# Hybrid attention/HGRN2 layer: per-head weight blocks for queries and keys, and attention taken one block at a time with the scores two blocks ahead

## The chip, the core and the metric

The kernel runs on one core of one Trainium2 chip. The metric is the device time of one execution in microseconds (us). The kernel before was run three times: 1170.23, 1170.86 and 1172.86 us, a median of 1170.86 us.

## What is computed

One layer on 1024 tokens of width 1024, in float32. Only the first half of it matters here:

```python
u = rms_norm(x, norm1_g)
aq, ak, av, hq, hf, hi, hg = split(u @ w_in)     # each 1024 x 512
attn = dilated_attention(aq, ak, av)             # 8 heads of 64
rec  = hgrn2_mixer(hq, hf, hi)                   # 4 recurrent heads of 128
h = x + concat(norm(attn), norm(rec) * silu(hg)) @ w_out
out = rms_norm(h + conv_glu(rms_norm(h)))
```

The attention has three causal windows merged by their softmax denominators: the last 128 keys, every fourth of the last 512, every sixteenth of the last 2048. For a block of 128 queries that is one softmax over up to 256 near keys (the block and the one before) and the far keys of the query's own residue modulo 4 (32 per earlier block), with a mask that carries the logarithm of how often a key is counted.

## The kernel before, in words

Every large product is made of three float32r matmuls: weights and activations are split into a high part (a cast on ScalarE, L87) and a low part (a subtraction on VectorE, L89), and high*high, high*low and low*high are added in PSUM (L492 to L494). The weights come through a ring (class `Ring`): a raw tile is loaded by a DMA on SyncE's queue, split, and used up by one step of 12 matmuls; five steps are kept ahead. Two 128-row blocks of `w_qk` together with two halves of the tokens are multiplied in seven steps instead of eight (Strassen-Winograd form): `PairMix` makes the weight sums on VectorE, `pair_block` (L511) runs the seven steps through two PSUM banks with the tag "mm" and adds their results into four tiles from `mtile` (tag "m", four buffers).

Only TensorE's order is written out by hand (`manual_schedule`); the other engines' orders are chosen by a scheduler when the program is built. TensorE is interleaved like this. `qk_block(0)` runs first. The other three pairs of heads, and the first HGRN2 projections (`early`, L784), are generators in `fill`; each `fill.run(us)` emits about so many us of their matmuls between pieces of the attention. For each pair of heads p (four of them) and each block b of 128 queries (eight):

- `scores(p, b)` (L690): 16 or 32 small matmuls into two PSUM banks S (one per head), then for each head the row minimum of mask minus scores with its write to P (VectorE, L715), the exponential with its sum (ScalarE, L717), the reciprocal (VectorE, L718) and the division (GpSimd, L719). P has two buffers per head.
- `turn(p, b)` (L724): transposes of P on TensorE into banks Tn and Tf of the tag "t" (L734, L742), copied out by ScalarE (pl, L735) and VectorE (far_t and tri, L745 and L748).
- `values(p, hf)` (L750), once per four blocks: the products with v into a bank O.

Blocks go in twos: scores of two blocks, values if four are complete, some fill, turn, fill, turn, fill. PSUM has eight banks: two each of "o", "t", "s" and "mm". Even blocks put their scores into "s" and "s", odd ones into "t" and "o". After the last block `fill.run()` empties what is left.

Queries and keys are laid out by `evac` (L632): each finished tile of a qk block holds one head, 64 rows of queries over 64 rows of keys. VectorE scales it by the norm of its tokens (L636), then ScalarE copies its two halves into the tiles qp and kp (L638), reordered so that within a block of 128 tokens those of one residue modulo 4 lie together. Four tiles per pair make 32 such copies in all.

`restore` (L776) reloads a quarter of x into four `mtile`s and rebuilds the operand T4, which the second half of `early` needs.

The functions around the change, with the line numbers of the profile:

Of the kernel before, what the change touches and what calls it, by code (L numbers as in the profile page):

```python
# [10 lines left out]
F32 = mybir.dt.float32  # L11
# [6 lines left out]
P = 128  # L18
SEQ = 1024
DM = 1024  # L20
NCT = DM // P
H2 = 512
NH = 8
# [4 lines left out]
KS = 4  # L28
# [111 lines left out]
class PairMix:  # L140


    def __init__(self, nc, a, b):
        self.nc, self.a, self.b, self.g0, self.g1 = nc, a, b, None, None

    def load(self, ring):
        self.g0, self.v0, self.v1 = ring.raw(self.a[:, 0:H2]), ring.raw(self.b[:, 0:H2]), ring.raw(self.b[:, H2:])

    def a11(self, ring):
        self.load(ring)  # L150
# [8 lines left out]
        return self.s  # L159

    def a12(self, ring):
        self.g1 = ring.raw(self.a[:, H2:])
        return self.g1

    def s3(self, ring):
# [81 lines left out]
def hybrid_kernel(ctx: ExitStack, tc: tile.TileContext, xT, w_qk, w_tok, w_hg, w_out, w_up,  # L247
                  w_down, vecs, amask, hmask, out):
    nc = tc.nc
    PE, DVE, ACT, POOL = nc.tensor, nc.vector, nc.scalar, nc.gpsimd  # L250
# [29 lines left out]
    halves = [slice(0, H2), slice(H2, SEQ)]  # L280
# [47 lines left out]
    def part(f, i):  # L328
        return w_up[f, :, H2 * i : H2 * (i + 1)]

    for f in range(NFF):
        if f < 2:
            plan += [((x, f), part(f, i)) for x, i in (("a11", 0), ("a12", 3), ("a21", 1), ("a22", 2))]
        else:
            m = Mix(nc, w_up[f])
# [3 lines left out]
    ring = Ring(nc, ringp, plan)  # L339
# [37 lines left out]
    R1 = ua.tile([P, SEQ], F32, name="R1")  # L377
# [10 lines left out]
    def bank(tag, name):  # L388
        return ps1.tile([P, H2], F32, tag=tag, name=name, bufs=2)
# [4 lines left out]
    at = at_cm.__enter__()  # L394
# [6 lines left out]
    ring.aside = {("a12", 1): None}  # L401

    def mtile(name):
        return at.tile([P, H2], F32, tag="m", name=name, bufs=4)

    def otile1(name):
        return at.tile([P, H2], F32, tag="ot", name=name, bufs=1)
# [6 lines left out]
    xp = xp_cm.__enter__()  # L414
# [8 lines left out]

    pin = tc.keep_in_program_order
    xt = {(hf, c): xs[hf][c // 2][:, (c % 2) * H2 : (c % 2 + 1) * H2] for hf in range(2) for c in range(KS)}
    xt |= {(0, KS + c): mtile(f"x21_{c}") for c in range(KS)}
    xt |= {(1, KS + c): xp.tile([P, H2], F32, name=f"x22_{c}") for c in range(KS)}
    OPS1 = ("B11", "B21", "T4", "B22")

# [136 lines left out]
    fill = Fill()  # L566
# [48 lines left out]
    for t in TURN:  # L615
        x = vtile(f"it{t}")
# [6 lines left out]
    qk = {}  # L623

    def by_residue(ap):
        return ap.rearrange("p (b l r) -> p b r l", l=32, r=4)

    def in_order(ap):
        return ap.rearrange("p (b r l) -> p b r l", l=32, r=4)

    def qk_evac(p):
        def evac(m, hf, src):  # L632
            if p not in qk:
                qk[p] = [at.tile([P, SEQ], F32, tag=x, name=f"{x}{p}", bufs=2) for x in ("qp", "kp")]
            t, r0 = halves[hf], 64 * m
            DVE.tensor_mul(src, src, R1[:, t])  # L636
            for dst, y in zip(qk[p], (slice(0, 64), slice(64, 128))):
                ACT.copy(in_order(dst[r0 : r0 + 64, t]), by_residue(src[y]))  # L638
        return evac

    def qk_block(p):
# [2 lines left out]
    FAR, NEAR = 192, 256  # L644
# [11 lines left out]
    ab = ab_cm.__enter__()  # L656
# [2 lines left out]
    tri = ab.tile([P, 2, 2, P], F32, name="tri")  # L659
    if True:  # L660
        nat = far_t.rearrange("p e b q -> p (e b q)")
        sel = ab.tile([P, FAR + NEAR], F32, tag="P0", name="sel", bufs=2)
        scratch = drv.tile([P, FAR + NEAR], F32, name="scratch")
        nat1 = ab.tile([P, FAR + NEAR], F32, tag="P1", name="nat1", bufs=2)
        nc.scalar.dma_start(nat1[:, 0:NEAR], amask[:, SEQ - NEAR :])
        nc.scalar.dma_start(nat[0:32, 0:768], amask[0:P:4, 0:768])
        POOL.tensor_scalar(in_order(sel[:, FAR:]), by_residue(nat1[:, 0:NEAR]), DH ** 0.5, 0.0, op0=ALU.mult, op1=ALU.add)
# [12 lines left out]
        def load_values(p, kb):  # L680
            near_v[p, kb] = ab.tile([P, 4, P], F32, tag="near", name=f"near{p}_{kb}", bufs=2)
            far_v[p, kb] = ab.tile([P, 4, P], F32, tag="far", name=f"far{p}_{kb}", bufs=2)
            src = vd[H2 * kb : H2 * (kb + 1), P * p : P * (p + 1)]
            for r in range(4):
                nc.sync.dma_start(near_v[p, kb][32 * r : 32 * r + 32], src.rearrange("(b l r) e -> r l b e", b=4, r=4)[r])
            nc.sync.dma_start(far_v[p, kb], src.rearrange("(p r) e -> p r e", r=4))
# [3 lines left out]
        def scores(p, b):  # L690

            qp, kp = qk[p]
            far = 32 * max(b - 1, 0)
            near = P if b == 0 else 2 * P
            k0 = (b + 1) * P - near
            n = far + near
            S = [bank(("to" if b % 2 else "ss")[e], f"S{p}_{b}_{e}") for e in range(2)]
            rows = [slice(64 * e, 64 * e + 64) for e in range(2)]
            k4 = kp.rearrange("p (b r l) -> p r b l", r=4, l=32)
            for part in range(2 if far else 1):  # L700
                for r in range(4):
                    o = slice(32 * r, 32 * r + 32)
                    for e in range(2):
                        q = qp[rows[e], b * P + 32 * r : b * P + 32 * r + 32]
                        if part == 0:
                            PE.matmul(S[e][o, far:n], q, kp[rows[e], k0 : k0 + near], start=True, stop=True)
                        else:
                            PE.matmul(S[e][o, 0:far].rearrange("p (b l) -> p b l", l=32), q,  # L708
                                      k4[rows[e], r, 0 : b - 1], start=True, stop=True)
            m = mask[:, FAR - far :] if b else mask[:, FAR + P :]  # L710
            Ps = probs[p, b] = []
            for e in range(2):
                Pt = ab.tile([P, FAR + NEAR], F32, tag=f"P{e}", name=f"P{p}_{b}_{e}", bufs=2)
                st = at.tile([P, 16], F32, tag="st", name=f"st{p}_{b}_{e}", bufs=8)
                DVE.tensor_tensor_reduce(Pt[:, :n], S[e][:, :n], m, -(DH ** -0.5), BIG * 3,  # L715
                                         op0=ALU.add, op1=ALU.min, accum_out=st[:, 0:1])
                ACT.activation(Pt[:, :n], Pt[:, :n], AF.Exp, bias=st[:, 0:1], scale=-1.0, accum_out=st[:, 2:3])  # L717
                DVE.reciprocal(st[:, 3:4], st[:, 2:3])  # L718
                POOL.tensor_scalar(Pt[:, :n], Pt[:, :n], st[:, 3:4], 1.0, op0=ALU.mult, op1=ALU.mult)  # L719
                Ps.append(Pt)  # L720
# [72 lines left out]
                if hf == 0:  # L793
                    restore()

        scores(0, 0)
        scores(0, 1)
        fill.add(early())
        us = 18.6
        ends = []  # L800
        for p in range(NH // 2):
            for j in range(4):
                if p or j:
                    for b in range(2):
                        scores(p, 2 * j + b)
                    while ends:
                        values(*ends.pop())
                if j == 0:
                    for kb in range(2):
                        load_values(p, kb)  # L810
                turns = [lambda b=b: turn(p, 2 * j + b) for b in range(2)] + [lambda: None]
                for n, f in zip(((3, 1, 1), (3, 2, 1), (2, 2, 1), (4, 3, 1))[j], turns):
                    fill.run(us / 24 * n)
                    f()
                if p == 3 and j == 3:
                    fill.run()
                if j % 2:
                    ends.append((p, j // 2))
        values(*ends.pop())
    ab_cm.__exit__(None, None, None)  # L820
    at_cm.__exit__(None, None, None)
# [2 lines left out]
    with pool("hg", "right") as hg:  # L824
# [95 lines left out]
        for hf in range(2):  # L920
            for kind, h in HG[0]:
                x = tile_of(kind, h, hf)
# [418 lines left out]
    with pool("ps2", "left", space=PSUM) as ps2:  # L1341
# [162 lines left out]
        for x, y in STAGES:  # L1504
# [27 lines left out]
            for d in range(KS):  # L1532
                src = ps[d]
# [89 lines left out]
```

## Time and profile before

| what | value |
| --- | --- |
| the profiled execution's own time | 1171.42 us |
| its span, first to last instruction | 1169.3 us |
| median of the three runs | 1170.86 us |
| TensorE matmuls, busy | 1145.6 us (98%) |
| weight loads, busy | 941.8 us (81%) |
| VectorE, busy | 923.7 us (79%) |
| ScalarE, busy | 604.3 us (52%) |
| GpSimd, busy | 87.5 us (7%) |
| chain that ended last | TensorE 86%, VectorE 7%, ScalarE 5% |
| the 32 copies of L638, busy | 17.8 + 18.1 us (in 95 to 282 us) |

A matmul of 512 columns is booked as busy for 0.39 us, but in a full stream the next one starts 0.23 us later; busy times of TensorE therefore overlap, and an idle time in the record begins only when the last booked time is over. The attention is the stretch from about 117 us (end of the first qk block) to 282.5 us (the end of the last values). In an idle entry such as `10.3 <-POOL P L719 5.1` the first number is the idle time ahead of a group of instructions, and what follows is the instruction whose end let it go on. DMA issues stand under SPq and ACTq, the queues of the engines that issue them.

### The profile page before, as it was taken

What the parts mean: (1) busy time and instruction counts of PE and PEld (TensorE: products, weight loads), DVE (VectorE), ACT (ScalarE), POOL (GpSimd) and SP (SyncE); (2) the same over time, 40 slices, a digit from 0 to 9 for tenths busy, and PEclk for the clock granted to TensorE, in tenths of its full rate; (3) what the DMA queues carried; (4) which work ended last, traced back from release to release, by engine and by line L of the source; (5) the groups of instructions that cost most, each with busy time, mean ns of one, the idle gap of its engine ahead of it and who ended that gap; (6) DMA issues with size and microseconds to landing.
All of it is one profiled execution on the core that took longest, in us unless ns stands there. A gap on an engine that the chain in (4) does not pass through costs nothing.

```text
span 1169.3 us, 17983 instructions
## 1 busy us (share of the span) xinstructions
PE 1145.6 (98%) x6472; PEld 941.8 (81%) x6472; DVE 923.7 (79%) x1728; ACT 604.3 (52%) x1149; POOL 87.5 (7%) x111
## 2 busy tenths in 40 slices
PE   9999899999999999999999999999999999999996
PEld 7887677778888888888788888888888888888886
DVE  7776667645876786759989998899888879857987
ACT  6545677654976665546434343434343344444553
POOL 5210122221000001120000000000000000000000
PEclk9999999999999999999999999999999999999998
DMA  6225121424212243340123333223322277435532
GB/s 245 87 67 165 38 92 47 129 81 147 91 55 64 72 155 124 110 135 27 55 89 101 117 127 108 81 100 117 117 90 83 97 255 250 135 99 162 168 106 88
DMA packets 84617, 130.90 MB, mean 112 GB/s; under 512 B 8432, under 2 KB 27664, under 8 KB 84528
## 3 DMA queue, kind: packets, MB, share of 16 engines
q1 hardware_dynamic: 70240, 105.08, 28.4%
q10 hardware_dynamic: 14288, 24.67, 5.6%
q8 instruction: 51, 0.84, 0.3%
q14 instruction: 38, 0.31, 0.1%
HBM read 98.63 MB, written 31.09 MB: 111 GB/s over the span
## 4 chain that ended last, share of the span: by engine, by line
PE 86%; DVE 7%; ACT 5%; issue 1%; DMA 1%; POOL 0%; ACTq 0%; SPq 0%; DVEq 0%; POOLq 0%
PE p L1224 10%; PE p L1223 10%; PE p L1222 10%; PE ds L1521 3%; PE ds L1523 3%; PE ds L1522 3%; PE po L492 3%; PE po L493 2%; PE po L494 2%; PE da L1521 2%; PE da L1523 2%; PE da L1522 2%; PE phq L492 1%; PE phg L492 1%; PE v L494 1%; PE phq L494 1%
## 5 line engine op out<-in xcount | busy, mean ns | idle before, releaser
L87 ACT CAST whi<-raww 128x512 fp32r<-128x512 f32 x246 | 150.5, 617 | 208.7 <-PE p L1223 69.0
L89 DVE TENSOR_TENSOR wlo<-raww,whi 128x512 fp32r<-128x512 f32 x247 | 173.1, 702 | 47.0 <-ACT whi L87 43.5
L87 ACT CAST whi<-r 128x512 fp32r<-128x512 f32 x70 | 43.6, 622 | 81.3 <-PE ds L1522 49.0
L89 DVE TENSOR_TENSOR wlo<-r,whi 128x512 fp32r<-128x512 f32 x70 | 48.0, 687 | 18.5 <-ACT whi L87 18.4
L1223 PE MATMUL p<-b1l,whi 128*128 128x512 f32 x160 | 62.3, 389 | 0.0
L1521 PE MATMUL ds<-fhi,whi 128*128 128x512 f32 x160 | 62.3, 389 | 0.0
L1522 PE MATMUL ds<-flo,whi 128*128 128x512 f32 x160 | 62.3, 389 | 0.0
L1224 PE MATMUL p<-b1h,wlo 128*128 128x512 f32 x160 | 62.3, 389 | 0.0
L1523 PE MATMUL ds<-fhi,wlo 128*128 128x512 f32 x160 | 62.3, 389 | 0.0
L1222 PE MATMUL p<-b1h,whi 128*128 128x512 f32 x160 | 62.3, 389 | 0.0
L89 DVE TENSOR_TENSOR flo<-rawf,fhi 128x512 fp32r<-128x512 f32 x70 | 48.0, 686 | 4.0 <-ACT fhi L87 3.9
L87 ACT CAST fhi<-rawf 128x512 fp32r<-128x512 f32 x70 | 43.1, 616 | 14.5 <-DMA rawf<-spT 5.8
L1495 POOL TENSOR_TENSOR facc<-facc,sqf 128x256 f32<-128x256 f32 x2 | 1.5, 739 | 637.3 <-ACT sqf L1494 637.3
L1251 ACT ACTIVATE cv<-cv 128x512 f32<-128x512 f32 x44 | 27.8, 632 | 40.6 <-DVE cv L1244 40.5
L1244 DVE SCALAR_TENSOR_TENSOR cv<-g,vec,cv 128x511 f32<-128x511 f32 (+2 forms) x92 | 44.7, 492 | 4.5 <-ACT cv L1241 4.2
L719 POOL TENSOR_SCALAR P<-P,st 128x128 f32<-128x128 f32 (+7 forms) x64 | 37.7, 591 | 132.8 <-DVE st L718 123.2
L1521 PE MATMUL da<-fhi,whi 128*128 128x512 f32 x120 | 46.7, 389 | 0.0
L1522 PE MATMUL da<-flo,whi 128*128 128x512 f32 x120 | 46.7, 389 | 0.0
L1523 PE MATMUL da<-fhi,wlo 128*128 128x512 f32 x120 | 46.7, 389 | 0.0
L717 ACT ACTIVATE P<-P,st 128x128 f32<-128x128 f32 (+7 forms) x64 | 35.7, 558 | 19.2 <-DVE st L715 19.0
L715 DVE CUSTOM_DVE_ANT_0 P<-S,mask 128x128 f32<-128x128 f32 (+7 forms) x64 | 30.0, 489 | 6.5 <-PE S L708 5.9
L1222 PEld LDWEIGHTS p<-b1h,whi 128*128 128x128 f32 x160 | 30.0, 188 | 6.3
(608 smaller groups left out, 3445.0 us busy)
## 6 DMA issues: line engine op xcount, KB each, us to landing
raww<-in_w_up_dram SPq DMA_DIRECT2D x88, 256.0 KB, 2.9
rawf<-spT SPq DMA_DIRECT2D x40, 256.0 KB, 2.7
r<-in_w_down_dram SPq DMA_DIRECT2D x40, 256.0 KB, 3.2
raww<-in_w_out_dram SPq DMA_DIRECT2D x32, 256.0 KB, 2.7
spB<-a ACTq DMA_DIRECT2D x30, 256.0 KB, 2.2
spT<-t ACTq DMA_DIRECT2D x30, 256.0 KB, 2.0
rawf<-spB SPq DMA_DIRECT2D x30, 256.0 KB, 2.7
raww<-in_w_hg_dram SPq DMA_DIRECT2D x24, 256.0 KB, 2.6
```

The lines of the kernel that those rows point to most:

```text
L87: self.pin(self.high(hi[:, :w], raw))
L89: self.pin(low.tensor_sub(lo[:, :w], raw, f32(hi[:, :w])))
L492: PE.matmul(ps, a[0], b[0], start=start, stop=False)
L494: PE.matmul(ps, a[1], b[0], start=False, stop=stop)
L719: POOL.tensor_scalar(Pt[:, :n], Pt[:, :n], st[:, 3:4], 1.0, op0=ALU.mult, op1=ALU.mult)
L1222: PE.matmul(ps, hi[:, s], bhi, start=(start and n == 0), stop=False)
L1223: PE.matmul(ps, hi[:, s], blo, start=False, stop=False)
L1224: PE.matmul(ps, lo[:, s], bhi, start=False, stop=(stop and n == len(rhs) - 1))
L1244: DVE.scalar_tensor_tensor(dst, x, col(V_CW + j * NFF + f), dst, op0=ALU.mult, op1=ALU.add)
L1521: PE.matmul(ps[d], hi[:, s], ahi, start=(k == 0), stop=False)
L1522: PE.matmul(ps[d], hi[:, s], alo, start=False, stop=False)
L1523: PE.matmul(ps[d], lo[:, s], ahi, start=False, stop=(k == NPAIR - 1))
```

## The change

It has two parts. In the first, each raw tile of `w_qk` is put together from two blocks, 64 columns of each (`PairMix.part`): its four 128-column groups hold one half of block a beside the same half of block b, so that a finished tile holds the queries of both heads of a pair, or the keys of both. Every tile is loaded by two DMAs in pieces of 256 bytes where it was one DMA with 2 KB per partition. `evac` then is one VectorE multiplication that reads in order and writes qp or kp in the reordered layout; the ScalarE copies go.

In the second, the attention goes block by block. The scores of blocks 0 and 1 are made ahead, and then in every slot n: the scores of block n + 2, fill, the values that are due, the turn of block n. For three sets of P alive at a time their buffers go from two to three; `mtile`s go from four to three, and one x tile moves to another pool. Odd blocks' scores go into "s" and "o" instead of "t" and "o".

```diff
+    def part(self, ring, s, x):
+        t = ring.raw()
+        t4 = t.rearrange("p (c m e) -> p c m e", c=KS, m=2)
+        for m, w in enumerate((self.a, self.b)):
+            w4 = w.rearrange("p (c s e) -> p c s e", c=NCT, s=2)
+            ring.order(self.nc.sync.dma_start(t4[:, :, m], w4[:, KS * x : KS * (x + 1), s]))
+        return t
...
-        self.g0, self.v0, self.v1 = ring.raw(self.a[:, 0:H2]), ring.raw(self.b[:, 0:H2]), ring.raw(self.b[:, H2:])
+        self.g0, self.v0, self.v1 = self.part(ring, 0, 0), self.part(ring, 1, 0), self.part(ring, 1, 1)
...
-        self.g1 = ring.raw(self.a[:, H2:])
+        self.g1 = self.part(ring, 0, 1)
...
-        return at.tile([P, H2], F32, tag="m", name=name, bufs=4)
+        return at.tile([P, H2], F32, tag="m", name=name, bufs=3)
...
-            t, r0 = halves[hf], 64 * m
-            DVE.tensor_mul(src, src, R1[:, t])
-            for dst, y in zip(qk[p], (slice(0, 64), slice(64, 128))):
-                ACT.copy(in_order(dst[r0 : r0 + 64, t]), by_residue(src[y]))
+            t = halves[hf]
+            nat = [x.rearrange("p (b l r) -> p b l r", l=32, r=4) for x in (src, R1[:, t])]
+            DVE.tensor_mul(qk[p][m][:, t].rearrange("p (b r l) -> p b l r", l=32, r=4), *nat)
...
-            S = [bank(("to" if b % 2 else "ss")[e], f"S{p}_{b}_{e}") for e in range(2)]
+            S = [bank(("so" if b % 2 else "ss")[e], f"S{p}_{b}_{e}") for e in range(2)]
...
-        scores(0, 0)
-        scores(0, 1)
         fill.add(early())
-        us = 18.6
+        slots = [(p, b) for p in range(NH // 2) for b in range(8)]
+        LAG = 2
+        for x in slots[:LAG]:
+            scores(*x)
+            fill.run(1.5)
         ends = []
-        for p in range(NH // 2):
-            for j in range(4):
-                if p or j:
-                    for b in range(2):
-                        scores(p, 2 * j + b)
-                    while ends:
-                        values(*ends.pop())
...
+        for n, (p, b) in enumerate(slots):
+            if n + LAG < len(slots):
+                scores(*slots[n + LAG])
+            if b == 0:
+                for kb in range(2):
+                    load_values(p, kb)
+            fill.run(1.2 if ends else 2.6)
+            while ends:
+                values(*ends.pop())
+            turn(p, b)
+            if b % 4 == 3:
+                ends.append((p, b // 4))
+        fill.run()
         values(*ends.pop())
```

Where the work stands after it can be read from the engines' built orders. On TensorE, before, around the turn of block 6 of the third pair of heads (phf is fill, Tn and Tf are that turn's transposes; the first number behind a name is the block, the last one a running number):

```order
L494 MATMUL phf_0_2671<-B11h,wlo_2313 128x512
L734 MATMUL Tn_6_2684<-ident,P_6_0_2616 128x128 x2
L734 MATMUL Tn_6_2684<-ident,P_6_1_2622 128x128 x2
L742 MATMUL Tf_6_2691<-ident,P_6_0_2616 128x128
L742 MATMUL Tf_6_2691<-ident,P_6_1_2622 128x128
...
L492 MATMUL phf_0_2671<-B21h,whi_2405 128x512
```

And with the change, around the same turn (S_1 are scores of block 1 of the next pair of heads):

```order
L503 MATMUL phf_0_2644<-B21h,wlo_2389 128x512
L742 MATMUL Tn_6_2702<-ident,P_6_0_2554 128x128 x2
L742 MATMUL Tn_6_2702<-ident,P_6_1_2560 128x128 x2
L750 MATMUL Tf_6_2709<-ident,P_6_0_2554 128x128
L750 MATMUL Tf_6_2709<-ident,P_6_1_2560 128x128
...
L714 MATMUL S_1_0_2716<-kp_2241,qp_2240 32x256
```

A turn stood between two pieces of fill; now it has fill ahead of it and the scores of two blocks later behind it. Over the whole attention, counted from these orders, scores are followed by fill 9 times before and 32 times now, by values 7 times and never; fill by scores 16 times and 3; turns by fill 30 times and never; turns by scores never and 29 times; values by fill 7 times and never, and by turns never and 7 times. At the very end two turns follow each other before and three now.

On ScalarE, before, around the exponentials of blocks 6 and 7 of the second pair (qp and kp the reordering copies, P the exponentials, pl the copies of a turn, whi a cast of weights):

```order
L638 COPY qp_1785<-u_10_1790 64x512
L638 COPY kp_1786<-u_10_1790 64x512
L717 ACTIVATE P_6_0_2074,st_6_0_2075<-P_6_0_2074,st_6_0_2075 128x416
L717 ACTIVATE P_6_1_2080,st_6_1_2081<-P_6_1_2080,st_6_1_2081 128x416
L717 ACTIVATE P_7_0_2104,st_7_0_2105<-P_7_0_2104,st_7_0_2105 128x448
L87 CAST whi_2124<-raww_1864 128x512
L717 ACTIVATE P_7_1_2110,st_7_1_2111<-P_7_1_2110,st_7_1_2111 128x448
L638 COPY qp_1785<-u_01_1622 64x512
L638 COPY kp_1786<-u_01_1622 64x512
L735 COPY pl_6_2144<-Tn_6_2143 128x512
```

And with the change, around the same exponentials:

```order
L725 ACTIVATE P_6_0_2023,st_6_0_2024<-P_6_0_2023,st_6_0_2024 128x416
L725 ACTIVATE P_6_1_2029,st_6_1_2030<-P_6_1_2029,st_6_1_2030 128x416
L743 COPY pl_4_2078<-Tn_4_2077 128x512
L725 ACTIVATE P_7_0_2106,st_7_0_2107<-P_7_0_2106,st_7_0_2107 128x448
L725 ACTIVATE P_7_1_2112,st_7_1_2113<-P_7_1_2112,st_7_1_2113 128x448
L87 CAST whi_2127<-raww_1700 128x512
L529 COPY u_00_2046<-w_2047 128x512
L743 COPY pl_5_2138<-Tn_5_2137 128x512
```

The copies qp and kp, which stood ahead of exponentials and of pl, are gone, and each pl comes right behind the exponentials of the block two further on.

More of the change, by code (lines that the diff above doesn't have):

```diff
@@ L425, in hybrid_kernel @@
     xt = {(hf, c): xs[hf][c // 2][:, (c % 2) * H2 : (c % 2 + 1) * H2] for hf in range(2) for c in range(KS)}
-    xt |= {(0, KS + c): mtile(f"x21_{c}") for c in range(KS)}
+    xt |= {(0, KS + c): mtile(f"x21_{c}") if c else xp.tile([P, H2], F32, name="x21_0") for c in range(KS)}
     xt |= {(1, KS + c): xp.tile([P, H2], F32, name=f"x22_{c}") for c in range(KS)}
@@ L661, in hybrid_kernel @@
         nat = far_t.rearrange("p e b q -> p (e b q)")
-        sel = ab.tile([P, FAR + NEAR], F32, tag="P0", name="sel", bufs=2)
+        sel = ab.tile([P, FAR + NEAR], F32, tag="P0", name="sel", bufs=3)
         scratch = drv.tile([P, FAR + NEAR], F32, name="scratch")
-        nat1 = ab.tile([P, FAR + NEAR], F32, tag="P1", name="nat1", bufs=2)
+        nat1 = ab.tile([P, FAR + NEAR], F32, tag="P1", name="nat1", bufs=3)
         nc.scalar.dma_start(nat1[:, 0:NEAR], amask[:, SEQ - NEAR :])
@@ L712, in scores @@
             for e in range(2):
-                Pt = ab.tile([P, FAR + NEAR], F32, tag=f"P{e}", name=f"P{p}_{b}_{e}", bufs=2)
+                Pt = ab.tile([P, FAR + NEAR], F32, tag=f"P{e}", name=f"P{p}_{b}_{e}", bufs=3)
                 st = at.tile([P, 16], F32, tag="st", name=f"st{p}_{b}_{e}", bufs=8)
@@ L794, in early @@
                     restore()
-        scores(0, 0)
-        scores(0, 1)
         fill.add(early())
-        us = 18.6
-        ends = []
-        for p in range(NH // 2):
-            for j in range(4):
-                if p or j:
-                    for b in range(2):
-                        scores(p, 2 * j + b)
-                    while ends:
-                        values(*ends.pop())
[L808 to L818, printed above, removed]
+        slots = [(p, b) for p in range(NH // 2) for b in range(8)]
[3 more added lines that the diff above has]
+            fill.run(1.5)
+        ends = []
+        for n, (p, b) in enumerate(slots):
[11 more added lines that the diff above has]
+        fill.run()
         values(*ends.pop())
```

## The prediction

> **What bounds the kernel now.** I read the page, then the stages, then the waits of the attention stage, then single waits in the timeline. The stages first: start and end, busy time of TensorE, weight loads, VectorE, ScalarE and GpSimd, and behind them the granted TensorE clock.
>
> ```profile
> 117.00:282.50 165.50, 153.57 (x1861) 119.76 (x1859) 104.21 (x312) 105.35 (x222) 38.13 (x65) 0.98 0.25 79
> 282.50:1163.00 880.50, 877.32 (x4114) 727.84 (x4110) 733.32 (x1291) 435.17 (x820) 20.76 (x18) 1.00 0.35 114
> 128.70:132.10 3.40, 3.38 (x17) 1.67 (x23) 0.77 (x3) 1.35 (x3) 0.95 (x2) 0.50 0.27 77
> 227.70:231.10 3.40, 3.26 (x12) 2.62 (x11) 2.40 (x6) 2.78 (x6) 1.42 (x3) 0.50 0.46 172
> ```
>
> After 282.5 us TensorE idles 3.2 us in 880, so what the attention saves is handed on whole. In the attention (165.5 us) it idles 11.9 us, and in two stretches of 3.4 us its clock is 0.50. No other engine is near full: VectorE 63%, ScalarE 64%. So the bound is TensorE, and what can be won is its waits in this stage. This group and these waits of that stage say for what it waits (idle time behind the second bar; in the second fence the total, the times, the longest):
>
> ```profile
> L734 PE MATMUL Tn<-ident,P 128*128 128x128 f32 x120 | 21.1, 287 | 10.3 <-POOL P L719 5.1 <-ACT pl L735 4.8
> ```
>
> ```profile
> PE Tn L734 <- POOL P L719: 5.1, 6, 2.0
> PE Tn L734 <- ACT pl L735: 4.8, 5, 1.8
> PE w L492 <- ACT u L520: 0.8, 1, 0.8
> PE S L706 <- ACT pl L735: 0.6, 1, 0.6
> ```
>
> Nearly all of it is the turns: their transposes wait until GpSimd has divided P, or until ScalarE has emptied the turn bank. Why these are late shows in single rows of the timeline (start, duration, idle time in brackets), two waits for GpSimd and one for ScalarE:
>
> ```profile
> 127.67 0.68 PE L734 MATMUL Tn<-ident,P 128*128 128x128 f32 x2 [1.69 <-POOL P L719]
> ...
> 224.64 1.09 ACT L638 COPY kp<-u 64x512 f32<-64x512 f32 x1
> ...
> 227.40 1.28 PE L734 MATMUL Tn<-ident,P 128*128 128x128 f32 x4 [2.02 <-POOL P L719]
> ...
> 241.78 1.09 ACT L638 COPY kp<-u 64x512 f32<-64x512 f32 x1
> 242.78 0.57 ACT L735 COPY pl<-Tn 128x512 f32<-128x512 f32 x1
> 243.50 0.63 PE L734 MATMUL Tn<-ident,P 128*128 128x128 f32 x4 [1.80 <-ACT pl L735]
> ```
>
> In the two later ones ScalarE was at the reordering copies of L638, which stand in its queue ahead of what TensorE waits for: of the exponentials that GpSimd's division needs, and of pl. The first one has the same cause (its rows stand with the rivals).
>
> **The change part by part.** First what goes.
>
> (a) The turns' waits. A booked 512-column matmul lasts 0.39 us and its successor starts 0.23 later (rows below), so each wait counts 0.16 us too little: 10.3 + 11 x 0.16 = 12.1 us. The scores are now two slots ahead of their turn. A slot is some 165.5 / 32 = 5.2 us, where now only some fill lies between; the chain minimum, exponential, reciprocal, division needs one slot. And pl stands right behind the exponentials in ScalarE's order with a slot to the next turn. One wait, in the last two turns, has no fill and stays (0.4 + 0.16). Gone: 11.5 us.
>
> (b) The scores no longer use the turn banks (0.6 + 0.16), and the "mm" bank that waited for a ScalarE copy behind four L638 copies is free in time (0.8 + 0.16). Gone: 1.8 us.
>
> (c) The two half-clock stretches start 1.0 and 0.3 us after the two waits for GpSimd quoted above. At half speed 3.4 us hold 1.7 us of work: 2 x 1.7 = 3.4 us gone with the waits.
>
> [...] The rows decide for me: both stretches come right behind such a wait, and nowhere else before the end.
>
> Then what comes. The switches between small and large matmuls cost something, and the new order has others. These rows are fill, then scores, then fill; below the dots the end of the attention:
>
> ```profile
> 151.69 0.39 PE L493 MATMUL w<-B22l,whi 128*128 128x512 f32 x1
> 151.91 0.40 PE L494 MATMUL w<-B22h,wlo 128*128 128x512 f32 x1
> 152.24 0.66 PE L706 MATMUL S<-kp,qp 64*32 64x256 f32 x16
> 152.69 0.48 PE L708 MATMUL S<-kp,qp 64*32 64x160 f32 x16
> 152.96 0.64 PE L706 MATMUL S<-kp,qp 64*32 64x256 f32 x16
> 153.40 0.53 PE L708 MATMUL S<-kp,qp 64*32 64x192 f32 x16
> 153.86 0.50 PE L492 MATMUL w<-B22h,whi 128*128 128x512 f32 x1
> 154.19 0.40 PE L493 MATMUL w<-B22l,whi 128*128 128x512 f32 x1
> ...
> 276.25 0.39 PE L494 MATMUL phq<-B22h,wlo 128*128 128x512 f32 x1
> 276.49 0.60 PE L734 MATMUL Tn<-ident,P 128*128 128x128 f32 x4
> 276.92 0.60 PE L742 MATMUL Tf<-ident,P 128*128 128x128 f32 x4
> 277.91 0.63 PE L734 MATMUL Tn<-ident,P 128*128 128x128 f32 x4 [0.39 <-ACT pl L735]
> ...
> 282.43 0.28 PE L770 MATMUL O<-tri,far 96*64 96x64 f32 x4
> 282.65 0.50 PE L492 MATMUL phg<-B11h,whi 128*128 128x512 f32 x1
> 282.98 0.40 PE L493 MATMUL phg<-B11l,whi 128*128 128x512 f32 x1
> ```
>
> (d) Fill to scores takes 152.24 - 151.91 = 0.33 where the pace is 0.23: 0.10 too much. Scores to fill: the last 16 take 0.46 (153.40 to 153.86), where 160 columns took 0.27 and 192 should take 0.32, so 0.14; the first fill matmul then takes 0.33 for 0.23, another 0.10: together 0.24. Fill to a turn takes 0.24, nothing extra, and I count turn to fill as nothing too. Values to fill: 0.10 at the first matmul and about as much before it, 0.2. A turn followed by scores does not occur in this trace: it lies between 0 (fill to turn) and 0.24 (scores to fill); I take 0.10, the nearest being fill to scores. From the counts of the orders: scores to fill 9 to 32, +23 x 0.24 = +5.5; fill to scores 16 to 3, -1.3; turn to scores 0 to 29, +2.9; values to fill 7 to 0, -1.4; the switches into values taken alike. Sum +5.7 us, with the ends +2.8 and +9.8.
>
> (e) At the end three turns stand without fill. A bare turn took 277.91 - 276.49 = 1.42 us, where eight transposes at 0.43 per four take 0.87: one more costs 0.55 us (0.5 to 1.5, since the last P is also closer to its scores).
>
> (f) `restore` has three m tiles instead of four, and its casts stand in ScalarE's queue between exponentials; and at the very start the scores of block 2 wait for the row minima of block 1. The row for restore is the 3.5 us that ScalarE idles for x now:
>
> ```profile
> L781 ACT ACTIVATE T4h<-x,vec 128x512 fp32r<-128x512 f32 x4 | 2.9, 722 | 3.5 <-DMA x<-in_xT_dram 3.5
> L638 ACT COPY qp<-u 64x512 f32<-64x512 f32 x14 | 15.9, 1132 | 6.4 <-DVE u L636 6.2
> L636 DVE TENSOR_TENSOR u<-u,R 128x512 f32<-128x512 f32 x14 | 10.2, 729 | 0.0
> L87 ACT CAST whi<-raww 128x512 fp32r<-128x512 f32 x27 | 16.5, 615 | 5.1 <-PE w L493 2.3 <-PE phf L493 2.2 <-PE phq L493 0.2
> L772 DVE COPY ot<-O 128x512 f32<-128x512 f32 x8 | 5.5, 685 | 3.7 <-PE O L770 3.7
> ```
>
> Between 0 and 3.5 us for both; two slots of lead and T4's use five slots later cover most; I take 0.5.
>
> (g) Counted at nothing: ScalarE's copies, 15.9 us into qp and about as much into kp, are off TensorE's path except as in (a) and (b). The evac multiplication stays one per tile; it only writes in strides. VectorE's 104.2 us over 32 slots are 3.3 us of a slot of about 4.9. The weights' small pieces: a near relative, the far load in 512-byte pieces, lands in 3.3 us against 2.6:
>
> ```profile
> raww<-in_w_qk_dram SPq DMA_DIRECT2D x16, 256.0 KB, 2.6
> far<-vd SPq DMA_DIRECT2D x8, 256.0 KB, 3.3
> ```
>
> Two DMAs of half a tile each may need some 2 us more than now, with SyncE's second issue; the ring is five steps deep, and a step alone is 12 x 0.23 = 2.7 us, so 13 us lie between a refill and its use. Without that cover each of 12 loads of the stage would cost its 2 us.
>
> Sum: -11.5 - 1.8 - 3.4 + 5.7 + 0.55 + 0.5 = -10.0 us. The profiled execution took 1171.42 us, 0.56 more than the median of the runs; 1161.4 for it, 1160.9 for the median.
>
> **The rivals.**
>
> *Slower: the row minima hold up the scores.* Before, a pair of blocks used four banks, and the next pair came 10 us later. Now both blocks share "s", so the scores of each slot wait for the minima of the slot before. If VectorE is late by more than a slot less the scores' own 0.9 us, that is 4.0 us, each further 0.1 us costs 32 x 0.1 = 3.2 us; at 4.3 the 10 us are used up, at 4.6 it is 1180. For it:
>
> ```profile
> 121.78 0.88 PE L706 MATMUL S<-kp,qp 64*32 64x128 f32 x32
> 123.83 0.69 DVE L89 TENSOR_TENSOR wlo<-raww,whi 128x512 fp32r<-128x512 f32 x1 [3.41 <-ACT whi L87]
> 125.89 0.28 DVE L715 CUSTOM_DVE_ANT_0 P<-S,mask 128x128 f32<-128x128 f32 x1
> ```
>
> The first minima came 4.1 us after their scores. Against it: VectorE waited there 3.41 us for a cast that stood behind L638 copies, which go (121.78 is the first pair of scores, behind the first qk block). What could bring it back is the strided write: the ordered copies of ScalarE take 1.13 us for 512 elements against 0.62 of a plain cast, while VectorE's ot copy, which reads PSUM in strides, takes 0.69, no more than a plain one. Doubled, 16 multiplications add 16 x 0.73 = 11.7 us of VectorE's time, 0.7 in the slots that have one. [...] No row shows a VectorE write of that kind. Chance 0.11.
>
> *The waits move instead of going.* Half of (a) and (b) and one half-clock stretch remain, since the transposes still need GpSimd and pl: -6.6 - 1.7 + 6.7 = -1.6 us, 1169.3. For it: the banks of the turns are still two. Against it: the rows that made them late are copies that go. Chance 0.13.
>
> *More is won.* Turn to scores costs nothing and (f) is 0: -16.7 + 2.8 + 0.5 = -13.4, 1157.5. Chance 0.18.
>
> That the change does not do what it says is excluded by the built orders. Weights that come late (+2 us for each of 12 loads on top, about 1185) I give 0.03.
>
> **How the numbers follow.** The forecast (-6 to -12 us) has 0.55: 1160.9 us. The range goes from below the better rival (each of the waits taken is a lower count) to the middle one: 1154 to 1169. Outside it remain 0.14 for the two slow cases, and a little on either side. A measurement of this kernel can tell 0.2%, 2.3 us, from no change. Faster by more: 0.55 + 0.18 + 0.06 of the middle rival = 0.79; within: 0.08; slower: 0.13.
>
> **What would show it.** In the profile after: the stage that begins with the first scores ends near 272 us instead of 282.5; the rows Tn <- POOL and Tn <- ACT pl fall to under 1.5 us together; no stretch with the clock at 0.50 before the end; L638 is gone from ScalarE; the first fill matmul behind scores still takes 0.33. Wrong: S waiting for VectorE's L715 (now L723) in many slots, an evac of over 1.2 us, or weights (w <- whi or wlo) in the waits of TensorE.

## The result, and the profile after

| | before | after |
|---|---|---|
| median of the runs shown, us | 1171.19 (1170.23 to 1172.86, 4 runs) | 1159.49 (1158.89 to 1160.61, 4 runs) |
| profiled execution, us (its span) | 1171.42 (1169.3) | 1159.09 (1157.3) |
| first scores to the first fill matmul behind the last values, us | 160.87 | 148.46 |

The ratio is 0.990, with a 95% interval of 0.9883 to 0.9917. Forecast were 1160.9 us, 10.0 us less in the profiled execution; it is 12.3 less. The attention alone gives 12.4, so what follows it only moved up. These are its two rows (first the kernel before, then the changed one; columns as in the prediction's stages):

```profile
121.78:282.65 160.87, 148.94 (x1841) 116.15 (x1840) 101.11 (x307) 101.44 (x218) 38.13 (x65) 0.98 0.24 77
```

```profile
121.76:270.22 148.46, 147.53 (x1841) 114.30 (x1840) 104.55 (x306) 73.22 (x190) 43.27 (x65) 1.00 0.28 83
```

TensorE idled 11.9 us there and idles 0.9 now; the clock is 1.00; ScalarE lost 28 us of work; VectorE has 3.4 us more. On the page, the chain that ended last is nearly TensorE's alone (it was 86%, with 5% of ScalarE):

```profile
PE 94%; DVE 5%; ACT 1%; issue 0%; DMA 0%; ACTq 0%; DVEq 0%; SPq 0%
```

Next all that TensorE waits for in the attention, and the groups of pl and of the strided scaling (kp and qp):

```profile
PE Tn L742 <- ACT pl L743: 0.9, 2, 0.6
```

```profile
L743 ACT COPY pl<-Tn 128x512 f32<-128x512 f32 x28 | 16.4, 585 | 23.6 <-PE Tn L742 23.3
L646 DVE TENSOR_TENSOR kp<-u,R 128x512 f32<-128x512 f32 x7 | 8.0, 1148 | 0.0
L646 DVE TENSOR_TENSOR qp<-u,R 128x512 f32<-128x512 f32 x7 | 7.5, 1075 | 0.0
```

Nothing waits for GpSimd any more. Now pl waits for its transposes (23.3 us of ScalarE's idle time), where they waited for it. The strided scaling takes 1.11 us, half as much again as the 0.73 of before, and not double. The only waits left are in the three bare turns at the end:

```profile
262.96 0.60 PE L742 MATMUL Tn<-ident,P 128*128 128x128 f32 x4
263.39 0.38 PE L750 MATMUL Tf<-ident,P 128*128 128x128 f32 x2
264.38 0.63 PE L742 MATMUL Tn<-ident,P 128*128 128x128 f32 x4 [0.60 <-ACT pl L743]
264.84 0.65 PE L750 MATMUL Tf<-ident,P 128*128 128x128 f32 x4
265.82 0.63 PE L742 MATMUL Tn<-ident,P 128*128 128x128 f32 x4 [0.33 <-ACT pl L743]
```

The turns start 1.42 and 1.44 us after one another, with 0.77 and 0.49 us more than the pace of their transposes: 1.26 us for the end.

Last, the switches, in a slot of the changed kernel (turn, scores, fill):

```profile
129.42 0.38 PE L742 MATMUL Tn<-ident,P 128*128 128x128 f32 x2
129.73 0.66 PE L714 MATMUL S<-kp,qp 64*32 64x256 f32 x16
130.19 0.32 PE L716 MATMUL S<-kp,qp 64*32 64x64 f32 x16
130.43 0.50 PE L501 MATMUL w<-T3h,whi 128*128 128x512 f32 x1
130.77 0.39 PE L502 MATMUL w<-T3l,whi 128*128 128x512 f32 x1
```

The two transposes and the step to the scores take 129.73 - 129.42 = 0.31 us; at a pace of 0.11 (0.43 for four, from 262.96 to 263.39 above) they should take 0.22, so turn to scores costs 0.09. The first fill matmul behind the scores takes 0.34 instead of 0.23.

### The profile page after: what moved, and what is told of

Read it like the earlier page. It is cut to its first block, busy times and chain, and to the rows that moved or that the text cites. A ratio compares the mean times of both kernels' runs of the same rounds, so it can differ in the third digit from the quotient of the medians.

```text
span 1157.3 us, 17957 instructions
## 1 busy us (share of the span) xinstructions
PE 1144.8 (99%) x6472; PEld 939.9 (81%) x6472; DVE 929.4 (80%) x1728; ACT 570.1 (49%) x1117; POOL 91.2 (8%) x111
## 4 chain that ended last, share of the span: by engine, by line
PE 94%; DVE 5%; ACT 1%; issue 0%; DMA 0%; ACTq 0%; DVEq 0%; SPq 0%
PE p L1229 11%; PE p L1227 11%; PE p L1228 11%; PE ds L1528 3%; PE ds L1526 3%; PE ds L1527 3%; PE po L501 3%; PE po L503 3%; PE w L501 3%; PE po L502 3%; PE da L1528 2%; PE da L1526 2%; PE da L1527 2%; PE w L503 2%; PE w L502 2%; PE S L714 2%
## 5 line engine op out<-in xcount | busy, mean ns | idle before, releaser
L727 POOL TENSOR_SCALAR P<-P,st 128x128 f32<-128x128 f32 (+7 forms) x64 | 42.8, 674 | 113.4 <-DVE st L726 111.3
L725 ACT ACTIVATE P<-P,st 128x128 f32<-128x128 f32 (+7 forms) x64 | 35.6, 558 | 21.5 <-DVE st L723 21.4
L1527 PEld LDWEIGHTS ds<-flo,whi 128*128 128x128 f32 x160 | 30.0, 188 | 6.3
```

The costliest lines, as they stand in the source:

```text
L1527: PE.matmul(ps[d], hi[:, s], alo, start=False, stop=False)
```

## The experiments

All times are medians against the kernel before in the same comparison. From trace to trace the first scores come up to some 2 us earlier or later (121.76 us in the changed kernel, 123.53 in lead_one), by when the full clock begins at the start (see the last section), so beside the median stands the length of the attention in the profiled execution, from the first scores to the first fill matmul behind the last values, which that does not touch.

| run | median, us | ratio, 95% interval | attention, us |
|---|---|---|---|
| changed kernel | 1159.49 | 0.9883 to 0.9917 | 148.46 |
| copies_gone | 1157.39 | 0.9868 to 0.9895 | 145.91 |
| order_alone | 1163.66 | 0.9925 to 0.9952 | 152.33 |
| lead_one | 1161.19 | 0.9900 to 0.9927 | 149.51 |
| pairs | 1175.60 | 1.0022 to 1.0047 | 164.70 |
| pairs_banks | 1161.57 | 0.9904 to 0.9928 | 150.87 |
| evac_twice | 1165.57 | 0.9933 to 0.9961 | 149.17 |
| copies_gone_fill | 1156.09 | 0.9858 to 0.9884 | 145.48 |
| pairs_fill | 1156.78 | 0.9857 to 0.9887 | 147.01 |
| after_fill | 1164.17 | 0.9919 to 0.9946 | 151.64 |
| pairs_late_fill | 1155.69 | 0.9854 to 0.9887 | 144.39 |

My theory: TensorE waited because ScalarE's reordering copies stood ahead of the exponentials and of pl; with them gone the waits go, with the half clock behind them, and the new order costs its switches. The first rival: it is the lead of the scores that removes the waits.

**copies_gone** is the kernel before with the change's `part` and `evac`, and nothing else of it:

```diff
-        self.g0, self.v0, self.v1 = ring.raw(self.a[:, 0:H2]), ring.raw(self.b[:, 0:H2]), ring.raw(self.b[:, H2:])
+        self.g0, self.v0, self.v1 = self.part(ring, 0, 0), self.part(ring, 1, 0), self.part(ring, 1, 1)
-            for dst, y in zip(qk[p], (slice(0, 64), slice(64, 128))):
-                ACT.copy(in_order(dst[r0 : r0 + 64, t]), by_residue(src[y]))
+            DVE.tensor_mul(qk[p][m][:, t].rearrange("p (b r l) -> p b l r", l=32, r=4), *nat)
```

> The kernel before with one part of the change alone: the weight blocks of queries and keys of their own and the scaling that writes in residue order, so that the 28 reordering copies of ScalarE are gone; slots, lead, banks and buffers as before. Theory (the copies in ScalarE's queue are the cause): the waits of the turns for GpSimd and for pl fall from 9.9 to under 2 us, both half-clock stretches go, and as the new order's switches are not there, it is faster than the changed kernel: 1171.2 - 16.7 + 1.5 = 1156 us. Rival (it is the lead of the scores that counts): the waits for GpSimd stay at some 5 us in 6 places with their half clock, only those for pl and u go: -5.6 - 1.8, about 1164 us.

Measured 1157.39, and 15.0 us off the attention. What TensorE still waits for there:

```profile
PE Tn L742 <- POOL P L727: 1.6, 3, 1.0
PE Tn L742 <- ACT pl L743: 0.4, 1, 0.4
PE Tf L750 <- DVE tri L756: 0.3, 1, 0.3
```

Of 9.9 us for GpSimd and pl 2.0 are left, without any lead. The copies were the cause. The prediction left out that at its wait of 2.02 us ScalarE had also stood 2.87 us for an x of `restore`, until 222.75, ahead of the copies; in copies_gone it stands 2.72 us for it at the same place, until 214.84, and the turn behind it, at 218.06, waits 0.22.

**order_alone** is the changed kernel with these edits the other way round, so that the copies are back and the order of the slots, the banks and the third P buffer are all that is left of the change:

```diff
-            DVE.tensor_mul(qk[p][m][:, t].rearrange("p (b r l) -> p b l r", l=32, r=4), *nat)
+            DVE.tensor_mul(src, src, R1[:, t])
+            for dst, y in zip(qk[p], (slice(0, 64), slice(64, 128))):
+                ACT.copy(in_order(dst[r0 : r0 + 64, t]), by_residue(src[y]))
```

> The changed kernel with the reordering copies of ScalarE put back (weight blocks and scaling as before), so that the order of the slots, the lead, the banks and the third P buffer are the only part of the change. Theory: P is ready 8 to 11 us ahead of its turn in the changed kernel, a block's four copies take 4.5 us, so the waits for GpSimd go all the same, with their half clock; of those for pl, which stands behind the copies with one slot of 5 us, about half stay; the switches are paid: -6.1 - 3.4 - 2.8 + 4 = -8, about 1163 us. Rival (only the lead counts): as the changed kernel, 1159.5. Rival (only the copies count): the waits stay, 1171 to 1175.

Measured 1163.66, attention 152.33. Its waits:

```profile
PE O L762 <- ACT pl L735: 1.4, 1, 1.4
PE w L492 <- ACT u L520: 1.0, 1, 1.0
PE S L706 <- DVE st L715: 0.9, 1, 0.9
PE Tn L734 <- ACT pl L735: 0.9, 2, 0.6
```

The sum came out, one term of it did not: half of the waits for pl between turns was to stay, and none is left but the tail's 0.9 us; in their place stand three single waits, 3.3 us: two at 124 and 126 us, at the first slots, and one at 224 us, where values wait for a pl. So the order removes the waits as well, by another way. The two parts of the change are no sum: alone they take 15.0 and 8.5 us off the attention, together 12.4. Once the copies are gone, the new order costs 2.5 us.

**lead_one** is the changed kernel with one slot of lead:

```diff
-        LAG = 2
+        LAG = 1
```

> The changed kernel with the scores one slot ahead instead of two. Theory: the chain from scores to a divided P takes about 3.6 us and one slot with its fill lasts over 4, so one slot of lead is enough where no copies stand in ScalarE's queue: no new waits of the turns, 1159.5 us within 1.5. Rival (two slots are needed): the waits for GpSimd come back in many of the 32 slots, 0.3 to 1 us each, 1169 or more.

Measured 1161.19, attention 1.05 us longer; its waits:

```profile
PE Tn L742 <- POOL P L727: 1.0, 2, 0.5
PE Tn L742 <- ACT pl L743: 1.0, 1, 1.0
```

Two waits for GpSimd in 32 slots, at one slot and at the last. The median is 1.7 us above the changed kernel's, a little over the 1.5 allowed. The second slot of lead is worth about 1 us of attention.

**pairs** and **pairs_banks** ask whether the switches of term (d) cost anything. The scores of two blocks come together, every second slot, and the turns one by one between fill; those of the first three blocks are made ahead, with 1.0 of fill behind each:

```diff
-            if n + LAG < len(slots):
-                scores(*slots[n + LAG])
+            if n and b % 2 == 0:
+                for x in slots[n + 1 : n + 3]:
+                    scores(*x)
```

> The changed kernel with the scores issued two blocks at a time, every second slot, with turns one by one between fill, and three P buffers still: 16 fewer switches from scores to fill and 14 fewer from turns to scores, 14 more from turns to fill. S of the second block of a pair uses one bank of the turns or of the other pair. Theory (the switches between small and large matmuls cost what the rows show): 15 x 0.09 + 16 x 0.2 = 4.5 us less, about 1155. Rival (the switch costs are only a shift of booked starts): no change, 1159.5. Rival (the banks hold it up): S or Tn waits for banks 0.5 us in 16 places, 1163 or more.

Measured 1175.60, slower than before. I had left the banks as they were, so that both blocks of a pair want "s", and the second waits for the first one's row minima:

```profile
PE S L714 <- DVE st L723: 10.0, 15, 1.6
```

That is the slower rival of the prediction, made by hand: 15 waits. What they cost is more than their booked 10.0 us: from one matmul of scores to the next it takes 35.6 us over all of them, 19.4 more than in the changed kernel and 17.6 more than in pairs_banks, which has as many such steps (18.0). One of the waits, of 1.59 us, also has 3.4 us at half clock behind it, and the last turn waits 2.2 us for GpSimd. In pairs_banks one line more is changed:

```diff
-            S = [bank(("so" if b % 2 else "ss")[e], f"S{p}_{b}_{e}") for e in range(2)]
+            S = [bank(("ss" if b % 2 else "to")[e], f"S{p}_{b}_{e}") for e in range(2)]
```

> The run with scores in pairs once more with one thing changed: the second block of a pair takes a bank of the turns and an "o" bank, and the first both "s" banks, so that the two blocks of a pair share no bank. Theory (the pairs were slow only because the second block's scores waited for the first block's row minima; the switches cost what the rows show): the 19.4 us that S to S took more there go, and the attention lasts some 4.5 us less than in the changed kernel: 1155 us, about 1.3 less if the turns' bank makes some waits. Rival (the switches cost nothing): 1159.5. Rival (sharing the turns' banks costs as much as it frees): 1165 or more.

Measured 1161.57: neither theory's number. The waits for the minima are gone; new ones stand in the last two turns, which have no fill in between, and 6.86 us at half clock behind them:

```profile
265.05 0.66 PE L750 MATMUL Tf<-ident,P 128*128 128x128 f32 x4 [1.87 <-DVE far_t L753]
267.66 1.30 PE L742 MATMUL Tn<-ident,P 128*128 128x128 f32 x4 [1.95 <-POOL P L727]
...
265.82:272.68 6.86, 5.02 (x36) 4.37 (x38) 1.89 (x8) 1.75 (x5) 1.72 (x3) 0.50 0.11 36
```

From the end of the fill it takes 5.4 us more than in the changed kernel (13.53 us, of them 0.92 for scores, against 7.26), and the rest of the attention 2.9 us less.

**copies_gone_fill, pairs_fill, after_fill and pairs_late_fill** deal out the fill otherwise. The first of them is copies_gone with

```diff
-        us = 18.6
+        us = 18.0
-                    fill.run(us / 24 * n)
+                    fill.run(us / 24 * n + (3.0 if n == 3 and not (p or j) else 0))
```

> The kernel before with the copies gone (weight blocks and scaling of the change, order of before), and the fill dealt out otherwise: 3 us more ahead of the first turn of all, and 18.0 instead of 18.6 us for each four pairs, so that some is left for the last turns. Theory: of the 2.3 us of waits left there, those of the first pair (1.7 us with what the rows book too little) and about half of the 1 us at the end go: 1155 us, 4 us faster than the changed kernel. Rival: the first turn waits for something else than P, no change, 1157.4.

Measured 1156.09, attention 0.4 us shorter. The first pair waits no more, but two turns, one at 218 us and one at the end, wait 1.8 us for pl, where it was 0.4, and the last wait for tri is 0.57 us, where it was 0.32: TensorE idles 2.3 us in both versions, so nearly all of the gain went there.

In after_fill and pairs_fill one number is changed, in the changed kernel and in pairs_banks:

```diff
-            fill.run(1.2 if ends else 2.6)
+            fill.run(1.2 if ends else 2.37)
```

> The changed kernel with fill.run(2.37) instead of 2.6 per slot, so that fill is left between the last three turns. Theory (term e: bare turns at the end cost what their rows show, 0.77 + 0.49 us): 1.3 us less, 1158.2. Rival (less fill per slot makes other waits): no gain or a loss.

> The run with scores in pairs and banks of their own, with fill.run(2.37) instead of 2.6 per slot, so that fill is left between the last three turns. Theory (its body is 4.3 us shorter than that of the changed kernel, as the switch costs foretold, and its end lost 8 us: two bare waits of 2.1 us and 6.8 us at half clock): the waits at the end and the half clock go, attention of about 143 us instead of 148.5, 1154 us. Rival (the end is slow for the pairs themselves): the last turns still wait for P, 1158 or more.

The waits at the end are gone in both, as expected, and still after_fill took 1164.17. One new wait stands in its attention, with a stretch at half clock behind it:

```profile
227.47 0.45 PE L714 MATMUL S<-kp,qp 64*32 64x128 f32 x16 [3.04 <-DVE kp L646]
...
228.80:232.30 3.50, 3.50 (x10) 2.58 (x9) 2.44 (x6) 2.63 (x7) 1.85 (x3) 0.51 0.41 124
```

The fill holds the query and key block of the last pair of heads. With less fill per slot it is not through when that pair's scores come, whatever the scores' own lead: -1.26 + 3.2 + 1.7 = +3.6 us, measured +3.2. The same wait stands in pairs_fill (2.13 us). The last version keeps 2.6 until that block is due:

```diff
-            fill.run(1.2 if ends else 2.6)
+            fill.run(1.2 if ends else 2.6 if n < 22 else 1.92)
```

> The run with scores in pairs and banks of their own, with the fill left at 2.6 per slot up to slot 21 and 1.92 from slot 22 on, so that the last query and key block is ready when its scores come (at 2.37 throughout its scores waited 2.1 us for the kp of VectorE) and fill still lies between the last turns. Theory: no wait of over 0.5 us is left, the attention lasts about 143 us against 148.5 in the changed kernel, 1154 us or a little less, faster than both kernels and than the run with less fill per slot. Rival (with 1.92 the last turns wait for P again): 1157 or more.

Measured 1155.69, 3.8 us below the changed kernel; attention 144.39. All its waits there:

```profile
PE Tf L750 <- DVE st L723: 0.4, 1, 0.4
PE Tn L742 <- ACT pl L743: 0.2, 1, 0.2
```

It beats both kernels. It has 14 switches fewer than the changed kernel from scores to fill (18 for 32) and from turns to scores (15 for 29), by term (d)'s rows some 4 us; its attention is 4.1 us shorter, 0.3 of it from shorter waits. So the switches do cost time. Against copies_gone_fill (1156.09) its interval does not set it apart.

**evac_twice** does the strided scaling of each tile two times. Its edit holds a second change, which its expectation does not name: ahead of the down projection, far behind the attention, a loop that prepares an operand and a weight by turns runs two times instead of four:

```diff
+            for _ in range(2):
-            DVE.tensor_mul(qk[p][m][:, t].rearrange("p (b r l) -> p b l r", l=32, r=4), *nat)
+                DVE.tensor_mul(qk[p][m][:, t].rearrange("p (b r l) -> p b l r", l=32, r=4), *nat)
...
-        for _ in range(4):
+        for _ in range(2):
             feed.fill(1)
             ring.fill(1)
```

> The changed kernel with the strided scaling of each query and key tile done twice by VectorE, so 1.1 us more in each slot that has one (16 in all). Theory: the row minima begin at most 1.7 us behind their scores, and the bank is wanted again some 4.2 us behind the end of the scores, so VectorE has over 2 us to spare in each slot: same as the changed kernel within 1.5 us. Rival (the minima of VectorE are near the point where they hold up the scores): up to 16 x 1.1, about 1175.

Measured 1165.57, 6.1 us above the changed kernel, where the theory had 0 and the rival 16. In the attention there are only 0.7 us (149.17), one wait for the minima of 0.3 us among them; another 1.0 lies ahead of the first scores (first scores at 124.54, in lead_one, which starts as late, at 123.53). The rest is 680 us further on (the first two rows are VectorE's):

```profile
935.98 2.49 DVE L89 TENSOR_TENSOR wlo<-r,whi 128x512 fp32r<-128x512 f32 x4
...
953.15 0.69 DVE L210 TENSOR_TENSOR r<-r,r 128x512 f32<-128x512 f32 x1 [3.55 <-DMA r<-in_w_down_dram]
...
955.10 0.58 PE L1528 MATMUL da<-flo,whi 128*128 128x512 f32 x1 [1.81 <-DVE flo L89]
...
955.30:958.71 3.41, 3.41 (x9) 2.65 (x9) 2.75 (x5) 0.00 (x0) 0.00 (x0) 0.51 0.69 177
```

In the down projection a flo of VectorE (the low part of an operand) came late, and a stretch at half clock followed: from the end of the attention to the last instruction it takes 891.6 us, 4.5 more than in the changed kernel. This is the stage of the second change. VectorE's order there is kept as the program writes it (`keep_in_program_order`), and it follows the loop: in the changed kernel four flo alternate with wlo, here two do, and four wlo come in a row behind them. The late flo stood in VectorE's queue behind a sum that had waited 3.55 us for a load of weights. That the 4.5 us come from this changed order is therefore likely, but the loop was not tried alone. So the median of 1165.57 says nothing of the scaling by itself. The attention does, as it lies ahead of that stage: 1.1 us more on VectorE do not reach the point where the minima hold up the scores (0.3 us of wait in all).

**stalls** and **stalls_again** are the changed kernel with P of eight blocks held back by further multiplications by 1 on GpSimd:

```diff
+                for _ in range({4: 19, 7: 20, 10: 25, 13: 21, 16: 31, 19: 24, 22: 22, 25: 34}.get(8 * p + b, 0) if e else 0):
+                    POOL.tensor_scalar(Pt[:, 0:P], Pt[:, 0:P], 1.0, 1.0, op0=ALU.mult, op1=ALU.mult)
```

> The changed kernel with P of eight blocks (4, 7, 10, 13, 16, 19, 22, 25) held back by 19 to 34 further multiplications by 1 on GpSimd, so that TensorE stands still before single turns for about 0 to 5 us, 12 us apart. My theory of the clock: a wait of TensorE of some 1.7 us or more is followed by 3.4 us at half speed, a shorter one mostly is not. [...] The time is 1159.5 + the stalls + 1.7 for each that is followed by half speed.

> The run with stalls once more with other counts of multiplications (20, 19, 31, 23, 31, 20, 21, 36), so that the stalls are some 1.5 to 2.5 us and begin elsewhere. Theory of a fixed grid: all half-clock stretches so far begin a whole multiple of 3.41 us apart within an execution (99.0 us is 29 of them, 64.7 is 19, 85.3 is 25) and last one or two; a step of this grid that holds about 1.7 us or more of waiting is followed by one at half speed. So a stall of 1.7 to 2.5 us that lies within one step is followed by 3.4 us at half speed, and one that is split by a border into parts under 1.6 us is not. Rival (the length of the wait alone decides): the same length always gives the same.

They took 1183.94 and 1182.1 us. Four waits, two of each run, and the granted clock behind them (0.50 or 1.00, third from the right):

```profile
167.28 0.58 PE L752 MATMUL Tf<-ident,P 128*128 128x128 f32 x3 [2.34 <-POOL P L730]
216.13 0.33 PE L744 MATMUL Tn<-ident,P 128*128 128x128 f32 x1 [2.11 <-POOL P L730]
...
167.75:171.16 3.41, 3.41 (x38) 2.48 (x38) 1.92 (x8) 1.15 (x4) 0.90 (x2) 0.51 0.02 5
216.20:219.60 3.40, 3.40 (x44) 2.66 (x45) 2.17 (x7) 2.10 (x6) 0.85 (x2) 1.00 0.71 216
```

```profile
231.88 0.44 PE L744 MATMUL Tn<-ident,P 128*128 128x128 f32 x2 [1.78 <-POOL P L730]
267.36 0.44 PE L744 MATMUL Tn<-ident,P 128*128 128x128 f32 x2 [1.94 <-POOL P L730]
...
233.16:236.57 3.41, 3.41 (x33) 2.37 (x19) 2.32 (x6) 1.86 (x6) 0.88 (x2) 0.50 0.22 84
267.40:270.80 3.40, 3.40 (x44) 2.58 (x45) 1.81 (x7) 2.06 (x6) 0.93 (x2) 1.00 0.01 4
```

Over both runs, waits of 2.34, 2.41 and 4.14 us, and of 2.00, 2.67, 1.78 and 1.95, were followed by half clock; 1.17, 1.47, 1.64, 2.11 (stalls) and 2.10, 1.94 (stalls_again) were not. So length alone does not decide: 1.78 did and 2.11 did not. The fixed grid explains those two: in stalls_again the stretches begin at 151.24, 181.96, 233.16 and 250.22, which are 9, 15 and 5 steps of 3.41 apart; in stalls at 167.67, 232.52 and 253.00, 19 and 6 steps; in the kernel before the two are 99.0 us apart, 29 steps. By this grid 2.11 is split by a border at 215.5 into 1.4 and 0.7, 2.10 by one at 216.1 into 0.9 and 1.2, and 1.64 and 1.47 are split too, while each of the seven that were followed has 1.7 us or more in one step. The 1.94 speaks against the threshold I had set: about 1.9 of it lie in one step, and the clock stayed. The other traces, each laid on its own grid, add to this. Of the steps at full clock, none with up to 1.43 us of idle time was followed by half clock, and all ten with 1.95 us or more were (idle meaning not covered by any booked matmul). Of the six between, 1.59 (pairs), 1.71, 1.78 and 1.81 were, and 1.80 (the wait before 243.5 in the kernel before) and 1.86 were not. In two steps that were at half clock themselves, 0.51 and 0.61 us were followed by a second one. Where between 1.43 and 1.95 us the threshold of these traces lies, and whether the kind of matmuls in the rest of the step counts, stays open.

## Why the prediction held, step by step

- **What bounds, (a) and (b).** Right, and the cause is shown: copies_gone takes the waits away without the new order. Forecast gone 11.5 + 1.8; what is left is only the tail. The waits of before were larger than the 12.1 us of the prediction: its 10.3 us are fourteen idle times, three of them too short for the list of waits, where it added 0.16 us for eleven; and the last turn's wait for tri (0.3 + 0.16 us, the row below) stands in none of its terms. From start to start, over the pace of the matmuls, they come to 13.0 us.

```profile
PE Tf L742 <- DVE tri L748: 0.3, 1, 0.3
```

- **(c) The half clock.** Right: both stretches are gone, and the stalls show that waits of this length bring them: seven of the 13 above were followed by half clock, the shortest of 1.78 us. The prediction read it as "right behind such a wait"; the runs add the grid of 3.41 us, which also accounts for some of the waits that were not followed by one. It does not account for the 1.80 at 243.5, whose row the prediction shows too: that wait lies whole within one step, and the clock stayed at 1.00 behind it.
- **(d) The switches.** Right in sign, the term that was mis-sized: +5.7 forecast, 4.4 measured. In the changed kernel against copies_gone the attention is 2.55 us longer, though its waits are 1.86 us less (3.12 us over the pace of their matmuls there, 1.26 here); so the order costs 2.55 + 1.86 = 4.4. Turn to scores is 0.09 each (forecast 0.10). Scores to fill is less: scores took 22.7 us in the changed kernel and 21.4 in copies_gone, 1.3 for 16 more separate groups, and the first fill matmul takes 0.11 more 23 times, 2.5: 3.8 where I had 23 x 0.24 = 5.5. The 0.14 that I read into the end of a group of scores is mostly there between two groups as well. Values to fill is 0.11, not 0.2, since the extra lies in the first fill matmul alone. 3.8 - 13 x 0.10 + 29 x 0.09 - 7 x 0.11 = 4.3.
- **(e) The end.** 1.26 us for what stays of (a) and the third turn together; forecast 0.56 + 0.55. Right.
- **(f) First slots and restore.** Too high: forecast 0.5, found 0, with no wait of TensorE in the changed kernel's attention but the two at the end.
- **(g) Counted at nothing.** Right. The strided write cost 1.11 - 0.73 = 0.38 us per tile, and VectorE had it to spare. Each half of a load, from its own issue, landed no later than the whole had (2.6 us for 256 KB before), and TensorE waits for none of them in the attention; the 2 us of delay that I had put behind the cover are shown by no run:

```profile
raww<-in_w_qk_dram SPq DMA_DIRECT2D x32, 128.0 KB, 2.5
```

The sum with what was measured: 13.0 of waits at the turns, 1.8 and 3.4 gone, 4.4 and 1.3 come, makes -12.5 where the attention lost 12.4. As 4.4 was taken from the difference to copies_gone, the test of this sum is copies_gone against before: 13.0 + 1.8 + 3.4 - 3.1 = 15.1, measured 15.0. The forecast of -10.0 had put the waits 0.9 us too low, the switches 1.3 and (f) 0.5 too high, and the end 0.15 too low. Nearly all of it points one way, so the forecast did not come near by errors that cancel; it was too cautious.

Of the rivals, *slower* did not happen, and pairs shows its mechanism to be real once two blocks share "s" without fill between them. *The waits move instead of going* does not hold for the whole change nor for the copies alone; with the order alone 3.3 us of waits stand in new places, and the half-clock stretches are gone. *More is won* named the wrong reason: turn to scores does cost, and the result lies between it and the forecast. What the prediction did not ask is whether both parts are needed. They are not: the copies gone are worth more alone than together with this order. The lead itself is not what costs: with the scores ahead in pairs (pairs_late_fill) the attention is shorter than in both.

## What to carry to other kernels

When TensorE waits for a chain over other engines, look first for what stands ahead of that chain in their queues, and take that away; a longer lead treats the same waits a second time, and taken block by block it costs switches between small and large matmuls, here 4.4 us. Test the parts of a change one by one: two cures of one wait don't add up. Read the whole edit of a run before you explain what it did far away: evac_twice changed the loop of the very stage that got slower. And spread the filler work to its deadlines, the next block's inputs and the last bare turns, since here eight of the ten waits of 2 us or more in the traces of the attention also brought 3.4 us or more at half clock (0.50), 1.7 us of time for each 3.4.

## What the runs showed of the hardware that was not expected

In the 14 traces the record of the full clock begins at 4.4 to 6.2 us in eight (5.82 in the kernel before, 6.21 in the changed one), and at 9.8 to 10.7 us in six, where the first scores come some 2 us later. In the changed kernel's profiled execution the fill pace of 0.23 is there from 6.58 us:

```profile
6.58 0.39 PE L501 MATMUL v<-whi,B11h 128*128 128x512 f32 x1
6.80 0.39 PE L502 MATMUL v<-wlo,B11h 128*128 128x512 f32 x1
```

In lead_one's it comes 3.6 us later, and the first scores at 123.53 instead of 121.76:

```profile
9.81 0.52 PE L502 MATMUL v<-wlo,B11h 128*128 128x512 f32 x1
10.17 0.40 PE L503 MATMUL v<-whi,B11l 128*128 128x512 f32 x1
```

One execution of each kernel was traced, so that this also makes the spread between executions of one kernel is not shown; it fits copies_gone, whose spans of 1156.2 and 1156.6 us have a mean clock of 0.997, and those of 1154.1 and 1154.5 one of 0.998. So differences of about 2 us between single executions say nothing, and lengths are best taken from a point behind the start.

A VectorE multiplication of 128x512 that writes 128 bytes apart takes 1.11 us against 0.73 for one that writes in a row; the prediction's range went from nothing to double.
